# Attention with low parts and masks formed by adding transfers, and a reordered end, in a one-core encoder block

## The chip, the cores and the metric

The kernel runs on one core of a Trainium2 chip. The metric is the device time of one execution in microseconds; the time before is the median of three runs, and one further execution was profiled. The engines are named as in the profile: PE (TensorE) multiplies matrices, DVE (VectorE) and ACT (ScalarE) do elementwise work and can read PE's banks, POOL (GpSimd) does elementwise work on on-chip memory only and issues transfers, and SP issues transfers. All five run their own queue of instructions in a fixed order.

## The reference

One layer over 512 positions of width 1024, in float32. Cut to what matters here:

```python
h = rmsnorm(x, norm_mix_g);  z = h @ w_in           # u, v, q, k, v, f_logit, gates
a = gmlp_spatial_gating(z_u, z_v, ...)              # 8 groups
for i in range(4):                                  # query blocks of 128, 16 heads of 64
    s = q_i @ k[:hi].T * 64**-0.5 + cum_i[:, None] - cum[None, :hi]
    s = where(kpos <= qpos, s, -1e30)
    o_i = softmax(s) @ v[:hi]
x = x + (gate_a * (a @ w_branch_a) + gate_b * (o @ w_branch_b)) @ w_out
x = x + (gelu(conv(up)) * conv(up)) @ w_down        # gated MLP, causal depthwise conv
x = x + (p @ w_ple) * sigmoid(rmsnorm(x) @ w_ple_gate)
return rmsnorm(x, norm_final_g)
```

`cum` is the running sum of log sigmoid(f_logit + b_f) of each head.

## The kernel before

**Two parts for each operand.** PE multiplies in a reduced float32 (fp32r in the profile). Weights and activations are therefore split into a high part (`hi`, the value rounded by a copy on ACT) and a low part (`lo`, the value less its high part), and a product is three matmuls: lo x hi, hi x lo, hi x hi (`mm3`, L166 to L169, and `proj_T_steps`, L171 to L186). `load_w` (from L145) loads a weight piece of 128 x 1024 from HBM on SP's queue into a `raw` buffer, writes `hi` on ACT (L153), and forms `lo` in one of three ways: a subtraction on DVE (L159, the default), the same on POOL (`sub=G`), or `sub="dma"`: ACT writes minus `hi` into `lo` (L156), and a transfer that POOL issues adds `raw` to it (L157). There are three `raw` buffers and a ring of five `hi`/`lo` pairs. The up-projection uses the third way throughout.

**The order of the work.** PE's order is written out by hand in every stage: generators yield after each matmul, and `weave` mixes them. The other queues are filled by a scheduler that runs a model of the chip when the kernel is built; it takes an instruction when its inputs are there in the model, earlier ones first, and so can move one ahead of what stands in front of it in the program. Within `tc.manual_schedule(engines=...)` the engines named keep the order of the program.

**Attention.** Eight pairs of heads. In the pass for pair `pr`, PE interleaves three things: the transposes of that pair's probabilities and their product with v; the scores of pair `pr+1`; and, as filling, the projections of q and k for pair `pr+2` (two weight pieces) and those of one gate or, in the last pass, two (one weight piece each). For each head and query block, `softmax_head` lets PE form the scores in one of two `sc` banks, DVE adds the row of `cum` and takes the minimum (L849 for the diagonal block with the mask in `md`, L853 for the others with `cum`), and ACT takes the exponential (L856). DVE scales the four blocks of a head by the reciprocal sums (L863). `transpose_head` transposes them into one of three `pt` banks, from where ACT copies the high part `pth` (L380) and DVE forms the low part `ptl` (L381); the fourth transpose of a head needs the bank of the first. `cum_pair` loads the two rows of `cum` of a pair, spread over all 128 partitions, with one transfer on SP, and POOL adds the mask block (0 or 1e30) to a copy of all four key blocks, `md` (L831; one buffer for both heads). The low parts of the q and k weights of pairs 2 to 7 are formed on POOL, those of pairs 0 and 1, of the gates, and of the two first pieces of `w_branch_b` on DVE.

**The end.** The last stage multiplies by `w_ple_gate`, in two halves of the columns, four blocks of 128 rows each. `evac_gate` (L1313) follows each block: `add_ple` takes the sigmoid on ACT, multiplies and adds on DVE (L1297, L1298) and forms the sum of squares (L449 on ACT); POOL multiplies by the final gain (`times_g`, L1306). After the second half POOL adds the two sums (L1320), divides and adds epsilon (L1321) and finds the reciprocal root by three Newton steps (`rsqrt_of`, L397 to L403); ACT scales the low half of the row block (L1323), DVE the high half (L1324), and one transfer on SP stores it. The last row block's second half is cut into two of 256 columns; its root is taken on ACT with one Newton step on DVE (`rstd_of`, L386 to L390), its halves are scaled on ACT (L1360) and DVE (L1362) and stored from ACT's and SP's queues.

Of the kernel before, what the change touches and what calls it, by code (L numbers as in the profile page):

```python
# [15 lines left out]
P = 128  # L16
# [27 lines left out]
def hybrid_block(  # L44
# [338 lines left out]
    def rstd_of(ms, eps_scale):  # L383

        a, sd, y, t = tiny("ra"), tiny("rsd"), tiny("ry"), tiny("rt")
        A.activation(sd, ms, AF.Sqrt, scale=eps_scale, bias=epst)  # L386
# [3 lines left out]
        V.tensor_scalar(y, t, 1.5, y, ALU.add, ALU.mult)  # L390
        return y
# [262 lines left out]
    def gate_weights(n):  # L654
        return load_w(w_in_v[:, :, gate_col(n):gate_col(n) + P], 8, P)
# [13 lines left out]
    def qk_weights(pr):  # L669
        return [load_w(w_in_v[:, :, c0 + P * pr:c0 + P * pr + P], 8, P, sub=G if pr > 1 else V)  # L670
                for c0 in (2048, 3072)]
# [154 lines left out]
    def cum_pair(pr):  # L826
        cum = att.tile([P, 2, S], F32, tag="cum", name=uid("cum"), bufs=2)
        nc.sync.dma_start(cum, bass.AP(tensor=cum_d.tensor, offset=cum_d.offset + 2 * pr * S,
                                       ap=[[0, P], [S, 2], [1, S]]))
        md = att.tile([P, 2, S], F32, tag="md", name=uid("md"), bufs=1)  # L830
        G.tensor_tensor(md.rearrange("p a (n k) -> p (a n) k", k=P),  # L831
                        cum.rearrange("p a (n k) -> p (a n) k", k=P),
                        maskb[:, None, :].broadcast_to([P, 2 * NB, P]), ALU.add)
        return cum, md

    def softmax_head(qk, cm, a, probs):

        qs_, ks_, kh = qk
        cum, md = cm
        rs = tiny("rs", NB, bufs=4)  # L840
        for i in range(NB - 1, -1, -1):
            n = P * (i + 1)
            qs = slice(P * i, P * i + P)
            bk = bank("sc")
            T.matmul(bk[:, :n], qs_[:, a, qs], ks_[:, a, :n], start=True, stop=False)
            T.matmul(bk[:, :n], qs_[:, a, qs], kh[:, a, :n], start=False, stop=True)
            t = att.tile([P, n], F32, tag=f"t{i}", name=uid(f"t{i}"), bufs=T_BUFS)
            mn = tiny("mn", 2, bufs=8)
            V.tensor_tensor_reduce(t[:, n - P:], bk[:, n - P:n], md[:, a, n - P:n],  # L849
                                   1.0, 3e38, ALU.add, ALU.min, mn[:, 0:1])  # L850
            m = mn[:, 0:1]
            if i:
                V.tensor_tensor_reduce(t[:, :n - P], bk[:, :n - P], cum[:, a, :n - P],  # L853
                                       1.0, mn[:, 0:1], ALU.add, ALU.min, mn[:, 1:2])
# [40 lines left out]
    def gate_early(n):  # L895
        return gate_steps(n, "mm", lambda: att.tile([P, S], F32, tag="ot", name=uid("gt"), bufs=1))
# [391 lines left out]
    def add_ple(bk, rb, c, tag):  # L1288
# [13 lines left out]
        V.scalar_tensor_tensor(bk, xr, 1.0, xr, ALU.mult, ALU.mult, accum_out=ss)  # L1302
        return ss

    def times_g(eng, rb, c):
        eng.tensor_tensor(ple[:, rb, c], x1[:, rb, c], gfin[:, c], ALU.mult)  # L1306

# [5 lines left out]
    def evac_gate(bk, rb, ch):  # L1313
        if ch == 0:
            half[rb] = add_ple(bk, rb, lo_c, "s0")
            times_g(G, rb, lo_c)
            return
        ss = add_ple(bk, rb, hi_c, "s1")
        times_g(G, rb, hi_c)
        G.tensor_tensor(ss, ss, half[rb], ALU.add)  # L1320
        G.tensor_scalar(ss, ss, 1.0 / D, EPS, ALU.mult, ALU.add)  # L1321
        y = rsqrt_of(ss, eng=G)
        A.activation(ple[:, rb, lo_c], ple[:, rb, lo_c], AF.Copy, scale=y)  # L1323
        V.tensor_scalar(ple[:, rb, hi_c], ple[:, rb, hi_c], y, None, ALU.mult)  # L1324
        nc.sync.dma_start(out_rows(rb, slice(0, D)), ple[:, rb, :])

    with tc.manual_schedule(engines={mybir.EngineType.PE}):
# [15 lines left out]

        rb = NB - 1
        r = ds(rb * P, P)
        parts = []
        for c0 in (0, 256):
# [5 lines left out]
            parts.append(add_ple(bk, rb, c, f"s{2 + c0 // 256}"))  # L1353
            if c0 == 0:
                V.tensor_tensor(half[rb], half[rb], parts[0], ALU.add)
# [4 lines left out]
        A.activation(ple[:, rb, lo_c], ple[:, rb, lo_c], AF.Copy, scale=y)  # L1360
        nc.scalar.dma_start(out_rows(rb, lo_c), ple[:, rb, lo_c])
# [37 lines left out]
```

## Time and profile before

| | |
|---|---|
| Median of three runs | 946.94 us (946.75 to 947.03) |
| The profiled execution | 946.21 us |
| Its span, first to last instruction | 944.4 us |
| Mean granted TensorE clock | 0.996 |
| Busy: PE, DVE, ACT, POOL | 98%, 66%, 55%, 16% of the span |
| Chain that ended last: PE, DVE, ACT, POOL | 89%, 5%, 2%, 1% |

The profile was taken of one execution. A row of a timeline gives the start in us from the start of the span, the length in us, the engine, the line in the kernel, the operation, the tiles it writes and reads, its size, how many instructions were merged, and in brackets how long the engine stood idle before it and what ended that. PE's matmuls are pipelined and their ends are modelled, so rows of PE overlap. A row of the busy time by stretch gives the stretch, its length, and the busy time of each engine in it with the number of instructions. A row of a group gives the count, the busy time and the mean length in ns, then the idle time before and what ended it.

### The profile page before, as it was taken

What the parts mean: (1) busy time and instruction counts of PE and PEld (TensorE: products, weight loads), DVE (VectorE), ACT (ScalarE), POOL (GpSimd) and SP (SyncE); (2) the same over time, 40 slices, a digit from 0 to 9 for tenths busy, and PEclk for the clock granted to TensorE, in tenths of its full rate; (3) what the DMA queues carried; (4) which work ended last, traced back from release to release, by engine and by line L of the source; (5) the groups of instructions that cost most, each with busy time, mean ns of one, the idle gap of its engine ahead of it and who ended that gap; (6) DMA issues with size and microseconds to landing.
All of it is one profiled execution on the core that took longest, in us unless ns stands there. A gap on an engine that the chain in (4) does not pass through costs nothing.

```text
span 944.4 us, 11947 instructions
## 1 busy us (share of the span) xinstructions
PE 923.5 (98%) x4327; PEld 765.1 (81%) x4327; DVE 625.6 (66%) x1104; ACT 521.7 (55%) x846; POOL 155.3 (16%) x160
## 2 busy tenths in 40 slices
PE   7999999999999998999999999999999999999995
PEld 6878888888888887888888888888888888888785
DVE  6787899557777888424554647667666767554844
ACT  7654675466666666433524566555565645444533
POOL 4000001352222101000001511110111101103125
PEclk9999999999999999999999999999999999999998
DMA  9523273753333321199842497684957764973202
GB/s 343 161 89 114 76 195 107 238 157 96 97 99 98 109 96 62 55 312 370 268 155 68 149 239 169 163 206 100 222 141 166 199 156 103 233 229 112 68 1 89
DMA packets 106376, 144.30 MB, mean 153 GB/s; under 512 B 5957, under 2 KB 71677, under 8 KB 106317
## 3 DMA queue, kind: packets, MB, share of 16 engines
q1 hardware_dynamic: 97740, 113.62, 37.7%
q0 software_dynamic: 8432, 29.66, 14.7%
q8 instruction: 34, 0.56, 0.3%
q14 instruction: 26, 0.20, 0.1%
q10 hardware_dynamic: 144, 0.26, 0.1%
HBM read 107.84 MB, written 14.71 MB: 130 GB/s over the span
## 4 chain that ended last, share of the span: by engine, by line
PE 89%; DVE 5%; ACT 2%; POOL 1%; issue 1%; DMA 1%; SPq 0%; POOLq 0%; DVEq 0%
PE bank L181 17%; PE bank L185 17%; PE bank L183 17%; PE bank L1190 8%; PE bank L243 3%; PE bank L247 3%; PE bank L245 3%; PE bank L317 3%; PE bank L313 3%; PE bank L320 3%; PE bank L168 2%; PE bank L169 2%; PE bank L167 2%; PE bank L883 2%; PE bank L874 1%
## 5 line engine op out<-in xcount | busy, mean ns | idle before, releaser
L181 PE MATMUL bank<-slot,wlo 128*128 128x512 f32 (+1 forms) x688 | 273.2, 398 | 0.0
L183 PE MATMUL bank<-slot,whi 128*128 128x512 f32 (+1 forms) x688 | 267.2, 389 | 0.0
L185 PE MATMUL bank<-slot,whi 128*128 128x512 f32 (+1 forms) x688 | 266.9, 389 | 0.0
L185 PEld LDWEIGHTS bank<-slot,whi 128*128 128x128 f32 x688 | 129.2, 188 | 26.7
L153 ACT CAST whi<-raw 128x1024 fp32r<-128x1024 f32 x105 | 109.8, 1048 | 70.3 <-PE bank L185 23.4
L181 PEld LDWEIGHTS bank<-slot,wlo 128*128 128x128 f32 x688 | 129.5, 188 | 21.5
L183 PEld LDWEIGHTS bank<-slot,whi 128*128 128x128 f32 x688 | 129.7, 189 | 20.5 <-DVE slot L381 0.2
L159 DVE TENSOR_TENSOR wlo<-raw,whi 128x1024 fp32r<-128x1024 f32 x51 | 63.0, 1238 | 46.0 <-ACT whi L153 45.6
L159 POOL TENSOR_TENSOR wlo<-raw,whi 128x1024 fp32r<-128x1024 f32 x21 | 51.3, 2447 | 194.4 <-ACT whi L153 186.8
L157 POOL DMA_DIRECT2D wlo<-raw x33 | 28.7, 871 | 222.5 <-ACT wlo L156 124.0
L1190 PE MATMUL bank<-whi,slot 128*128 128x512 f32 x192 | 61.7, 389 | 0.0
L243 PE MATMUL bank<-whi,slot 128*128 128x512 f32 x136 | 53.6, 396 | 2.0 <-DVE slot L381 2.0
L247 PE MATMUL bank<-whi,slot 128*128 128x512 f32 x136 | 53.2, 391 | 0.0
L245 PE MATMUL bank<-wlo,slot 128*128 128x512 f32 x136 | 52.9, 390 | 0.0
L1106 DVE SCALAR_TENSOR_TENSOR ul<-bank,cvT,ul 128x511 f32<-128x511 f32 x22 | 16.5, 750 | 46.3 <-ACT ul L1105 46.3
L1190 PEld LDWEIGHTS bank<-whi,slot 128*128 128x128 f32 x192 | 36.1, 188 | 7.4
L856 ACT ACTIVATE t<-t,mn 128x512 f32<-128x512 f32 (+1 forms) x64 | 35.9, 562 | 10.3 <-DVE mn L853 7.5
L380 ACT CAST pth<-bank 128x512 fp32r<-128x512 f32 (+1 forms) x64 | 26.2, 428 | 24.8 <-PE bank L874 24.6
L265 DVE TENSOR_TENSOR wlo<-slot,whi 128x1024 fp32r<-128x1024 f32 x24 | 29.3, 1222 | 15.7 <-ACT whi L264 15.7
L169 PE MATMUL bank<-whi,slot 128*128 128x512 f32 (+1 forms) x104 | 38.8, 373 | 0.0
L168 PE MATMUL bank<-wlo,slot 128*128 128x512 f32 (+1 forms) x104 | 38.8, 373 | 0.0
L167 PE MATMUL bank<-whi,slot 128*128 128x512 f32 (+1 forms) x104 | 38.7, 374 | 0.0
(327 smaller groups left out, 1812.3 us busy)
## 6 DMA issues: line engine op xcount, KB each, us to landing
raw<-in_w_up_dram SPq DMA_DIRECT2D x44, 512.0 KB, 4.3
raw<-in_w_in_dram SPq DMA_DIRECT2D x36, 512.0 KB, 5.2
wlo<-raw POOLq DMA_DIRECT2D x33, 512.0 KB, 5.4
more<-in_w_in_dram SPq DMA_DIRECT2D x20, 512.0 KB, 8.3
slot<-in_w_down_dram SPq DMA_DIRECT2D x16, 512.0 KB, 3.5
cum<-cum_d SPq DMA_DIRECT2D x8, 512.0 KB, 4.1
raw<-in_w_branch_b_dram SPq DMA_DIRECT2D x8, 512.0 KB, 3.8
slot<-aT_d SPq DMA_DIRECT2D x4, 1024.0 KB, 11.2
```

The source lines that it names most:

```text
L153: A.copy(hi, raw)
L159: (sub or V).tensor_tensor(lo, raw, hi.bitcast(F32), ALU.subtract)
L167: T.matmul(out_ap, alo, bhi, start=start, stop=False)
L168: T.matmul(out_ap, ahi, blo, start=False, stop=False)
L169: T.matmul(out_ap, ahi, bhi, start=False, stop=stop)
L181: T.matmul(out_ap, wl, ah, start=(n == 0 and k == 0), stop=False)
L183: T.matmul(out_ap, wh, al, start=False, stop=False)
L185: T.matmul(out_ap, wh, ah, start=False, stop=end)
L243: T.matmul(bk, alo[:, k, r], wh, start=(k == 0), stop=False)
L245: T.matmul(bk, ahi[:, k, r], wl, start=False, stop=False)
L247: T.matmul(bk, ahi[:, k, r], wh, start=False, stop=(k == nk - 1))
L1190: T.matmul(bk, l, m, start=(fresh and k == 0 and n == 0), stop=(k == 1 and n == 2), skip_group_check=not fresh)
```

## The change

In attention, the low parts of the q and k weights of pairs 2 to 7, of the gates from number 6 on, and of the first two pieces of `w_branch_b` are formed by the third way of `load_w` (ACT and an adding transfer). The masked rows `md` are loaded like `cum`, one head at a time, and the mask block is added to them by a transfer that POOL issues; `cum` shrinks to the 384 columns that are read; both have three buffers of one head each. None of POOL's additions and subtractions is left in that stage.

At the end, epsilon and the division by 1024 move into the first half's work (the scale of ACT's square, the factor on DVE, one addition on POOL), so that POOL's L1321 goes. The scaling and the store of the third row block are taken out of `evac_gate` and put behind those of the last row block; both its halves are scaled on ACT and its store goes out on ACT's queue. The last row block's halves are both scaled on DVE, high half first, and stored on SP's queue; its product with the gain comes after its scale; its root takes the last partial sum and the rest as two operands, so that one addition goes. ACT and DVE keep the order of the program there.

```diff
@@ rstd_of
-        a, sd, y, t = tiny("ra"), tiny("rsd"), tiny("ry"), tiny("rt")
-        A.activation(sd, ms, AF.Sqrt, scale=eps_scale, bias=epst)
+        a = tiny("ra")
         V.tensor_scalar(a, ms, -0.5 * eps_scale, -0.5 * EPS, ALU.mult, ALU.add)
+        return newton(a, ms, eps_scale, epst)
+
+    def newton(a, ms, scale, bias):
+        sd, y, t = tiny("rsd"), tiny("ry"), tiny("rt")
+        A.activation(sd, ms, AF.Sqrt, scale=scale, bias=bias)
         V.reciprocal(y, sd)
@@ qk_weights
-        return [load_w(..., 8, P, sub=G if pr > 1 else V)
+        return [load_w(..., 8, P, "dma" if pr > 1 else None)
@@ cum_pair
-        cum = att.tile([P, 2, S], F32, tag="cum", name=uid("cum"), bufs=2)
-        nc.sync.dma_start(cum, bass.AP(tensor=cum_d.tensor, offset=cum_d.offset + 2 * pr * S,
-                                       ap=[[0, P], [S, 2], [1, S]]))
-        md = att.tile([P, 2, S], F32, tag="md", name=uid("md"), bufs=1)
-        G.tensor_tensor(md.rearrange("p a (n k) -> p (a n) k", k=P),
-                        cum.rearrange("p a (n k) -> p (a n) k", k=P),
-                        maskb[:, None, :].broadcast_to([P, 2 * NB, P]), ALU.add)
-        return cum, md
+        res = []
+        for h in (2 * pr, 2 * pr + 1):
+            cum = att.tile([P, S - P], F32, tag="cum", name=uid("cum"), bufs=3)
+            md = att.tile([P, S], F32, tag="md", name=uid("md"), bufs=3)
+            for t, n in ((md, S), (cum, S - P)):
+                nc.sync.dma_start(t, bass.AP(tensor=cum_d.tensor, offset=cum_d.offset + h * S,
+                                             ap=[[0, P], [1, n]]))
+            G.dma_start(md.rearrange("p (n k) -> p n k", k=P),
+                        maskb[:, None, :].broadcast_to([P, NB, P]), accum_op=ALU.add)
+            res.append((cum, md))
+        return res
@@ gate_early
+        w = gate_weights(n, "dma" if n >= GATES[0] else None)
@@ preload_merge
-        w_merge.append(gate_weights(N_GATES - 1))
-        w_merge.append(pieces_T(w_b_v, 0))
+        w_merge.append(gate_weights(N_GATES - 1, "dma"))
+        w_merge.append(pieces_T(w_b_v, 0, "dma"))
@@ add_ple
+        ss = tiny(f"s{c.start // 256}", bufs=4)
         if n == 512:
-            return square_sum(bk, xr, tag)
-        ss = tiny(tag, bufs=4)
-        V.scalar_tensor_tensor(bk, xr, 1.0, xr, ALU.mult, ALU.mult, accum_out=ss)
+            A.activation(bk, xr, AF.Square, scale=D ** -0.5, accum_out=ss)
+        else:
+            V.scalar_tensor_tensor(bk, xr, 1.0 / D, xr, ALU.mult, ALU.mult, accum_out=ss)
         return ss
@@ evac_gate
-            half[rb] = add_ple(bk, rb, lo_c, "s0")
+            half[rb] = add_ple(bk, rb, lo_c)
+            G.tensor_scalar(half[rb], half[rb], EPS, None, ALU.add)
             times_g(G, rb, lo_c)
             return
-        ss = add_ple(bk, rb, hi_c, "s1")
+        ss = add_ple(bk, rb, hi_c)
+        G.tensor_tensor(ss, ss, half[rb], ALU.add)
+        y = rsqrt_of(ss, eng=G)
         times_g(G, rb, hi_c)
-        G.tensor_tensor(ss, ss, half[rb], ALU.add)
-        G.tensor_scalar(ss, ss, 1.0 / D, EPS, ALU.mult, ALU.add)
-        y = rsqrt_of(ss, eng=G)
-        A.activation(ple[:, rb, lo_c], ple[:, rb, lo_c], AF.Copy, scale=y)
-        V.tensor_scalar(ple[:, rb, hi_c], ple[:, rb, hi_c], y, None, ALU.mult)
-        nc.sync.dma_start(out_rows(rb, slice(0, D)), ple[:, rb, :])
+
+        def close(engs=(A, V), queue=nc.sync):
+            for c, eng in zip((lo_c, hi_c), engs):
+                times_y(rb, c, y, eng)
+            queue.dma_start(out_rows(rb, slice(0, D)), ple[:, rb, :])
+        rest[rb] = close
+        if rb < NB - 2:
+            close()
@@ the last row block, now under manual_schedule(engines={ET.PE, ET.Activation, ET.DVE})
-        V.tensor_tensor(half[rb], half[rb], parts[1], ALU.add)
-        y = rstd_of(half[rb], 1.0 / D)
+        a = tiny("ra")
+        V.tensor_scalar(a, part, half[rb], -0.5, ALU.add, ALU.mult)
+        y = newton(a, part, 1.0, half[rb])
         times_g(V, rb, c)
-        A.activation(ple[:, rb, lo_c], ple[:, rb, lo_c], AF.Copy, scale=y)
-        nc.scalar.dma_start(out_rows(rb, lo_c), ple[:, rb, lo_c])
-        V.tensor_scalar(ple[:, rb, hi_c], ple[:, rb, hi_c], y, None, ALU.mult)
+        times_y(rb, hi_c, y, V)
         nc.sync.dma_start(out_rows(rb, hi_c), ple[:, rb, hi_c])
+        times_y(rb, lo_c, y, V)
+        nc.sync.dma_start(out_rows(rb, lo_c), ple[:, rb, lo_c])
+        rest[rb - 1]((A, A), nc.scalar)
```

`times_y` scales one half of a row block by the block's scale, on ACT or on DVE.

More of the change, by code (lines that the diff above doesn't have):

```diff
@@ L652, in gate_col, with gate_weights @@
         return (6160 if n < NK else 5136) + P * (n % NK)
-    def gate_weights(n):
-        return load_w(w_in_v[:, :, gate_col(n):gate_col(n) + P], 8, P)
+    def gate_weights(n, sub=None):
+        return load_w(w_in_v[:, :, gate_col(n):gate_col(n) + P], 8, P, sub)
     def gate_tile():
@@ L669, in qk_weights @@
     def qk_weights(pr):
[L670 removed]
+        return [load_w(w_in_v[:, :, c0 + P * pr:c0 + P * pr + P], 8, P, "dma" if pr > 1 else None)
                 for c0 in (2048, 3072)]
@@ L895, in gate_early @@
     def gate_early(n):
-        return gate_steps(n, "mm", lambda: att.tile([P, S], F32, tag="ot", name=uid("gt"), bufs=1))
+        w = gate_weights(n, "dma" if n >= GATES[0] else None)
+        yield from gate_steps(n, "mm", lambda: att.tile([P, S], F32, tag="ot", name=uid("gt"), bufs=1), w)
     qk = [[] for _ in range(NPAIR)]
@@ L1306, in times_g, with times_y @@
         eng.tensor_tensor(ple[:, rb, c], x1[:, rb, c], gfin[:, c], ALU.mult)
+    def times_y(rb, c, y, eng):
+        if eng is A:
+            A.activation(ple[:, rb, c], ple[:, rb, c], AF.Copy, scale=y)
+        else:
+            V.tensor_scalar(ple[:, rb, c], ple[:, rb, c], y, None, ALU.mult)
     def out_rows(rb, c):
@@ L1342, in hybrid_block @@
         steps(pg, 72)
+    with tc.manual_schedule(engines={ET.PE, ET.Activation, ET.DVE}):
         rb = NB - 1
         r = ds(rb * P, P)
-        parts = []
         for c0 in (0, 256):
```

12 lines of the change are left out of this document (6 added, 6 removed).

## The prediction

> **What bounds the kernel now.** I read the page first, then the busy time by stretch, then who TensorE (PE) waits for, then the instructions around each of its stops, and last the end of the run.
>
> ```profile
> PE 923.5 (98%) x4327; PEld 765.1 (81%) x4327; DVE 625.6 (66%) x1104; ACT 521.7 (55%) x846; POOL 155.3 (16%) x160
> ```
>
> PE is busy for 923.5 of the span of 944.4 us, and the change takes no work from it. Only its 20.9 us of idle time can be won, and only the part that lies in the stages that the change touches. By stretch (length, then busy time of PE, weight load, DVE, ACT and POOL; clock; DMA share and rate):
>
> ```profile
> 205.00:220.00 15.00, 14.34 (x73) 11.71 (x72) 12.18 (x34) 9.95 (x23) 7.21 (x3) 1.00 0.49 141
> 220.00:350.00 130.00, 130.00 (x676) 108.77 (x675) 101.58 (x291) 86.10 (x193) 31.38 (x13) 1.00 0.33 96
> 350.00:378.00 28.00, 25.09 (x136) 20.26 (x135) 23.59 (x74) 18.82 (x48) 2.76 (x3) 1.00 0.22 70
> 925.00:944.40 19.40, 9.18 (x64) 8.39 (x62) 9.38 (x27) 7.04 (x14) 9.47 (x20) 0.79 0.28 109
> ```
>
> Attention runs from about 197 to 380. In its long middle PE has no idle time, although DVE is at 78% and ACT at 66%. PE is idle 0.66 us as attention gets going, 2.91 us in its last pairs, and 10.2 us at the end of the run. What PE waits for in attention (total, times, longest), and the rows at the stops:
>
> ```profile
> PE bank L874 <- DVE ptl L381: 3.2, 3, 1.7
> ```
> ```profile
> 216.66 0.33 PE L874 MATMUL bank<-ident,t 128*128 128x128 f32 x1 [0.66 <-DVE ptl L381]
> ...
> 358.21 0.39 PE L846 MATMUL bank<-kz,st 128*128 128x512 f32 x1
> 358.44 0.39 PE L181 MATMUL bank<-slot,wlo 128*128 128x512 f32 x1
> 360.55 0.33 PE L874 MATMUL bank<-ident,t 128*128 128x128 f32 x1 [1.72 <-DVE ptl L381]
> ...
> 376.01 0.33 PE L874 MATMUL bank<-ident,t 128*128 128x128 f32 x1 [0.87 <-DVE ptl L381]
> ```
>
> All three are the fourth transpose of a head, which needs the bank of the first back: ACT has to copy it (pth) and DVE to form its low part (ptl). Matmuls start 0.23 us apart (358.21, 358.44) but are drawn 0.39 long, so a stop is 0.16 us longer than its idle time: 0.82, 1.88 and 1.03 us. The remaining 0.3 us of idle time in 350 to 378 are two short stops near 367 and 369.
>
> **Why DVE is late there.**
>
> ```profile
> 211.31 4.70 DVE L863 TENSOR_SCALAR t<-t,ri 128x512 f32<-128x512 f32 x4
> ...
> 354.96 2.83 DVE L863 TENSOR_SCALAR t<-t,ri 128x512 f32<-128x512 f32 x4
> 357.83 0.69 DVE L892 TENSOR_TENSOR slot<-bank,ot 64x512 f32<-64x512 f32 x1
> 358.55 1.22 DVE L159 TENSOR_TENSOR wlo<-raw,whi 128x1024 fp32r<-128x1024 f32 x1
> 359.81 0.69 DVE L381 TENSOR_TENSOR ptl<-bank,pth 128x512 fp32r<-128x512 f32 x1
> ...
> 364.85 1.27 DVE L863 TENSOR_SCALAR t<-t,ri 128x512 f32<-128x512 f32 x4
> ```
> ```profile
> 210.40 2.40 POOL L831 TENSOR_TENSOR md<-cum,maskb 128x1024 f32<-128x1024 f32 x1 [0.86 <-PE bank L846]
> 213.51 2.42 POOL L159 TENSOR_TENSOR wlo<-raw,whi 128x1024 fp32r<-128x1024 f32 x1 [0.71 <-ACT whi L153]
> ...
> 354.32 2.40 POOL L831 TENSOR_TENSOR md<-cum,maskb 128x1024 f32<-128x1024 f32 x1 [21.64 <-DVE mn L849]
> ```
>
> The four scalings of a head (L863) take 1.27 us together at 364.85, 4.70 at 211.31 and 2.83 at 354.96. In the slow cases POOL is adding the mask or subtracting a low part, and the scaling that meets it stands until POOL has finished. So at 211 the loss is 3.43 us, at 355 it is 1.56 us, and there one more weight's low part (1.22 us) stands ahead of the ptl that PE needs.
>
> **The change in attention.** What goes, and what an adding transfer costs where the up-projection already uses it:
>
> ```profile
> L159 DVE TENSOR_TENSOR wlo<-raw,whi x12: 1222/1225/1228, 201.4 to 374.0; 128x1024 fp32r<-128x1024 f32 x12
> ```
> ```profile
> L159 POOL TENSOR_TENSOR wlo<-raw,whi 128x1024 fp32r<-128x1024 f32 x12 | 29.0, 2417 | 71.9 <-ACT whi L153 64.4 <-DVE st L822 7.5
> L831 POOL TENSOR_TENSOR md<-cum,maskb 128x1024 f32<-128x1024 f32 x8 | 19.2, 2400 | 48.6 <-issue 24.5 <-DVE mn L849 21.6 <-DMA cum<-cum_d 1.6
> ```
> ```profile
> L156 ACT ACTIVATE wlo<-whi x33: 1040/1060/1064, 537.5 to 831.6; 128x1024 fp32r<-128x1024 f32 x33
> ```
> ```profile
> L157 POOL DMA_DIRECT2D wlo<-raw x33: 860/869/915, 539.1 to 833.0; - x33
> DMA to landing us min/median/max: 4.6/5.3/8.8
> ```
>
> POOL loses all 48.2 us of arithmetic (29.0 + 19.2). DVE loses about a dozen low parts (9 gates, the last gate, two pieces of w_b): 12 x 1.225 = 14.7 us. ACT gains a negated copy for each of 24 weights: 24 x 1.06 = 25.4 us. POOL gains 24 issues of 0.87 us and 16 for the masks.
>
> At 216 DVE goes from the scalings (211.31 + 4.70) straight to the ptl that PE waits for; 3.43 us earlier, and the stop of 0.82 us is gone. At 358 DVE is 1.56 + 1.22 = 2.78 us earlier, more than 1.88, but now ACT decides:
>
> ```profile
> 357.45 0.57 ACT L380 CAST pth<-bank 128x512 fp32r<-128x512 f32 x1
> ```
>
> pth ends at 358.02, ptl takes 0.69, so the bank is free at about 358.8, and PE wants it at 358.67: nearly nothing is left. If one negated copy slips in front of pth, 1.06 us stay. I take 1.5 of 1.88. At 376 the last L159 on DVE (it starts at 374.0) goes, 1.23 against a stop of 1.03; with the same doubt about ACT I take 0.8. Of the two short stops I take 0.2, since pair 6 without a projection beside it leaves DVE nearly as long as PE. Together 0.82 + 1.5 + 0.8 + 0.2 = **3.3 us** (bounds: 0.8 if ACT takes over everywhere but at 216, 4.4 if all five go).
>
> Costed at nothing in the middle: ACT. In 130 us it goes from 86.1 by about 18 (17 copies) to some 104, 80%, which is where DVE stands today without stopping PE; and DVE gets slack in return. Also at nothing: the longer way of a low part. Two ACT passes, an issue and a landing are 2.1 + 5.3 = 7.4 us against 2.3, but the ring holds five weights and each feeds 24 matmuls of 0.23 us, 5.4 us of PE alone. If that cover were gone, a weight could be up to 5 us late. SP's three more loads a pair find the DMA engines at a share of 0.33.
>
> What can cost something is the very first mask, which now is a load and then an adding transfer:
>
> ```profile
> 197.29 0.29 DVE L849 CUSTOM_DVE_ANT_0 t<-bank,md 128x128 f32<-128x128 f32 x1 [0.93 <-POOL md L831]
> ```
> ```profile
> 197.45 0.33 PE L845 MATMUL bank<-st,st 128*128 128x384 f32 x1
> ...
> 199.63 0.28 PE L845 MATMUL bank<-st,st 128*128 128x256 f32 x1
> ```
>
> DVE waits 0.93 us for the mask already; PE does not stop, because its third score step, at 199.63 (the second is at 197.45), is the first that needs a bank back, one L849 and one L853 on DVE after the mask, about 1 us. The mask may thus be 1.4 us later than now, at 198.7. I know the adding transfer only with 512 KB and rows of 4 KB (4.6 to 8.8 us to land); here it is 256 KB in pieces of 512 bytes. POOL's addition of 2.40 us ended as DVE began, so the load had landed by 194.9; the half-size load should land a microsecond or two sooner, 193 to 194.8. With 4.6 the mask is there at 197.6 to 199.4, with 8.8 at 201.8 to 203.6: a stop of 0 to 0.7, or of 3 to 5. A gain is excluded, as PE doesn't stop there now. I take 0.4, by the lower row, since half the bytes move. For later heads three buffers give the mask over a head of lead (the scalings of two heads in turn are 9.9 us apart, 354.96 and 364.85). [...]
>
> **The change at the end.**
>
> ```profile
> 936.25 0.14 DVE L1302 DVE_READ_ACCUMULATOR bank<-slot 128x1 f32 x1
> 936.25 0.42 DVE L1306 TENSOR_TENSOR slot<-slot,slot 128x256 f32<-128x256 f32 x1
> 937.55 0.48 DVE L1324 TENSOR_SCALAR slot<-slot,qy 128x512 f32<-128x512 f32 x1 [0.89 <-POOL qy L403]
> ...
> 939.00 0.21 DVE L390 TENSOR_SCALAR ry<-rt,ry 128x1 f32<-128x1 f32 x1
> ```
> ```profile
> 937.55 0.72 ACT L1323 ACTIVATE slot<-slot,qy 128x512 f32<-128x512 f32 x1 [1.43 <-POOL qy L403]
> 938.18 0.28 ACT L386 ACTIVATE rsd<-s,epst 128x1 f32<-128x1 f32 x1
> 939.25 0.72 ACT L1360 ACTIVATE slot<-slot,ry 128x512 f32<-128x512 f32 x1 [0.79 <-DVE ry L390]
> 940.00 0.37 ACTq L1361 DMA_DIRECT2D out_dram<-slot  x1
> ```
> ```profile
> 933.22 0.42 POOL L1321 TENSOR_SCALAR s<-s 128x1 f32<-128x1 f32 x1
> ```
>
> The last square sum is there at 936.39, but both engines then stand before the third block's scale, which POOL has ready at 937.5, and the root starts only at 938.18. Now the root starts at about 936.4; root to finished scale took 939.21 - 938.18 = 1.03; then follow, on DVE in written order, the product with g (0.42) and two halves (0.48 each): the high half's store goes out near 938.3, the last one near 938.8, against 940.00. The third block's halves now run one after the other on ACT, 2 x 0.72 after 937.5 less the 0.4 that L1321 took out of POOL's chain: its store goes out at 938.5 to 939.0. So the last issue comes 1.0 to 1.4 us sooner. I take **1.2 us**, bounds 0.7 (the 512 KB store of block 2, now last, lands later than a 256 KB one) and 1.5.
>
> Sum: -3.3 + 0.4 - 1.2 = -4.1 us, a span of 940.3. The profiled execution took 946.21 with a span of 944.4; the median is 946.94, 0.7 above it. I take the difference off the median: **942.8**.
>
> **Rivals.** *ACT takes DVE's place* in the last pairs: negated copies stand before pth. For it: ACT is at 18.82 of 28 there and each copy is 1.06 us; against: ACT has 9 us free. Attention then gives 1.1, the whole 1.1 + 1.2 = 2.3: 944.6.
>
> *The issues stand in DVE's way as the additions did.* The rows show a scaling held by POOL's arithmetic, none beside an issue. At 0.87 an issue is shorter than the 1.56 and 3.43 lost, so the stops at 216 and 358 would still go; but 40 issues fall where only 20 operations did, and one on the scalings of each of the last two heads costs 2 x 0.87: -4.1 + 1.7, 944.5. [...]
>
> *The first mask is late* as by the 8.8 us row: a stop of about 3 us, once: 945.4.
>
> *Slower*: POOL issues in order, and a mask's add queued behind a weight's add waits until ACT has made both passes, which wait until PE has left a ring slot. DVE's first minimum of the head then waits, and PE stops at its third score step. It decides once the mask comes so late that the step after the next (2.2 us apart, 197.45 and 199.63) finds no bank; with 1.3 us beyond that in each of seven pairs it is 9.1 - 4.5 = +4.6, 951.5. Against it: three buffers let the add be issued a head ahead.
>
> **How the numbers follow.** Forecast 0.62, ACT 0.12, issues 0.09, late first mask 0.10, slower 0.07. The measurement tells 0.2%, 1.9 us, from no change, so faster means under 945.0. The forecast and about half of the two middle cases are faster: 0.73; the other half and the late mask lie within: 0.20; slower 0.07. The range runs from all stops gone and the best end (-4.4 - 1.5, 941.0) to the weak bounds of both parts with the mask's 0.4 on top (-0.8 - 0.7 + 0.4, 945.8), past the late mask.
>
> **What would show it.** No POOL arithmetic between 190 and 380; L863 at 1.3 us for every head; PE's wait for ptl in attention under 1 us; ACT near 80% in the middle and PE still without idle time; the first L849 waiting under 2 us; the last square root at 936.4 less the shift, and the last store 2.5 us behind it. I am wrong if PE waits for pth, md or wlo in attention, or if the third block's scale still ends last.

## The result and the profile after

| | before | after |
|---|---|---|
| Median, us | 946.85 (946.51 to 947.03, 4 runs) | 983.27 (981.58 to 983.73, 4 runs) |
| The profiled execution, its span | 946.21, 944.4 | 981.58, 979.8 |
| Mean granted TensorE clock | 0.996 | 0.981 |

The ratio of after to before is 1.0382, with a 95% interval of 1.0364 to 1.04: the change makes the kernel slower, by 36 us. In the changed kernel the lines from attention on have moved: the mask's adding transfer is L840, the loads of `cum` and `md` are L837, the minima L858 and L862, the scalings L872, the transposes L883, the copy of an attention output L900. The first part of the profile's page of after:

```profile
PE 934.0 (95%) x4327; PEld 772.8 (79%) x4327; DVE 600.5 (61%) x1091; ACT 544.2 (56%) x870; POOL 149.8 (15%) x181
```

PE is busy for 10.5 us longer with the same 4327 matmuls, and idle for 45.8 us instead of 20.9: 10.5 + 24.9 is the 35.4 us by which the span grew. DVE lost 25 us of work and ACT gained 22; neither is the bound.

What PE waits for in attention (total, times, longest), and the rows at one of the stops:

```profile
PE bank L883 <- DVE ptl L381: 26.5, 6, 10.7
PE bank L854 <- DVE mn L862: 2.8, 1, 2.8
```
```profile
285.74 0.47 PE L883 MATMUL bank<-ident,t 128*128 128x128 f32 x1 [4.52 <-DVE ptl L381]
...
288.36 0.63 PE L183 MATMUL bank<-slot,whi 128*128 128x512 f32 x1
288.79 0.63 PE L185 MATMUL bank<-slot,whi 128*128 128x512 f32 x1
...
290.58 0.40 PE L185 MATMUL bank<-slot,whi 128*128 128x512 f32 x1
290.81 0.28 PE L854 MATMUL bank<-st,st 128*128 128x256 f32 x1
```

The wait is the one of before, at the fourth transpose of a head, but 26.5 us in place of 3.2, and it now comes once in nearly every pass. For a while after the stop the matmuls start 0.43 us apart (288.36, 288.79), later 0.23 (290.58, 290.81), as in the rows of before (358.21, 358.44).

Taking the same matmul in both traces, one can say where after falls behind. It starts attention 0.6 us late and loses 3.0 at the first mask. The stop at 216 goes, which gives back 0.8. Then the stops come: 1.4 us at 257, and 4.7, 4.3, 2.4 and 4.0 at 285.7, 316.0, 344.6 and 374.0, and 10.6 at 403. The stops are 28.5 to 30.3 us apart up to 374, where the same transposes were 24.0 apart before (252.65, 276.60, 300.54). Of the 36.3 us that PE is behind at its end another 8.6 are time at the slower clock. The forecast gains are in it as well: 0.8 at 216, 1.7 where 360.55 was, 1.0 where 376.01 was, some 3.5 in all.

**Who stands behind the late ptl.** What ACT, the queue of SP and POOL wait for between 190 and 425:

```profile
ACT ot L900 <- DMA gate_d<-gt: 19.8, 5, 11.3
ACT whi L153 <- DMA raw<-in_w_in_dram: 18.5, 5, 5.0
```
```profile
SPq L150 <- DMA wlo<-raw: 171.0, 24, 13.6
```
```profile
POOL md L840 <- DMA md<-cum_d: 67.3, 8, 12.6
```

SP stands for 171 us, 24 times, because the next weight's load needs a `raw` buffer from which an adding transfer still has to read; POOL stands for 67 us because a mask's load has not landed. The two wait for each other. The queues of SP, POOL and ACT ahead of the stop at 285.74, in their own order:

```profile
273.39 0.38 SPq L150 DMA_DIRECT2D raw<-in_w_in_dram  x1
273.87 1.25 SPq L837 DMA_DIRECT2D cum<-cum_d  x1
275.22 0.42 SPq L837 DMA_DIRECT2D md<-cum_d  x1
276.38 0.38 SPq L150 DMA_DIRECT2D raw<-in_w_in_dram  x1
276.85 0.53 SPq L671 DMA_DIRECT2D gate_d<-gt  x1
289.51 0.38 SPq L150 DMA_DIRECT2D raw<-in_w_in_dram  x1
```
```profile
281.96 1.42 POOL L840 DMA_DIRECT2D md<-maskb  x1 [12.52 <-DMA md<-cum_d]
282.89 1.40 POOL L157 DMA_DIRECT2D wlo<-raw  x1
```
```profile
278.21 1.05 ACT L153 CAST whi<-raw 128x1024 fp32r<-128x1024 f32 x1 [4.40 <-DMA raw<-in_w_in_dram]
...
283.77 0.58 ACT L900 COPY ot<-bank 64x512 f32<-64x512 f32 x1 [1.92 <-DMA gate_d<-gt]
284.38 1.24 ACT L380 CAST pth<-bank 128x512 fp32r<-128x512 f32 x3
```

At 273.39 SP gets a `raw` buffer (an adding transfer landed at 273.34) and issues a weight's load; behind it stand the loads of `cum` and `md`. POOL has stood for 12.52 us for that mask and issues its add at 281.96; behind it, in POOL's order, stands a weight's add, although its weight landed at 264.14 and ACT was done with it at 267.56. That add lands at 289.49, and at 289.51 SP gets the next `raw` buffer. This is one **trip**: weight load, mask load behind it, mask add, weight add behind it, the next weight load. It took 16.1 us, the next one 13.4 (to 302.93), and there are two in a pass, one for each head's mask. So a pass takes 29.5 us, while PE needs 24.0. PE notices through ACT, which in the order of its queue waits for the weight (4.40 us) and then, to copy an attention output into the only `ot` buffer, for the landing of the gate's store that stands behind a waiting load (1.92); `pth` and `ptl` come behind that.

**The end.** The scaling of the third row block, which waits for POOL's root, and the last store of after:

```profile
974.07 1.33 ACT L1321 ACTIVATE slot<-slot,qy 128x512 f32<-128x512 f32 x2 [1.25 <-POOL qy L407]
975.43 0.37 ACTq L1344 DMA_DIRECT2D out_dram<-slot  x1
```

PE's last matmul ends at 970.50, against 934.18 before, so the last store is issued 4.93 us behind it instead of 5.82, and the run ends 9.3 us behind it instead of 10.2: 1.0 us won. How much of that the stores won is taken up with the end alone, below.

### The profile page after: what moved, and what is told of

Its sections match the earlier page's. It is cut to its first block, busy times and chain, and to the rows that moved or that the text cites. A ratio compares the mean times of both kernels' runs of the same rounds, so it can differ in the third digit from the quotient of the medians.

```text
span 979.8 us, 12091 instructions
## 1 busy us (share of the span) xinstructions
PE 934.0 (95%) x4327; PEld 772.8 (79%) x4327; DVE 600.5 (61%) x1091; ACT 544.2 (56%) x870; POOL 149.8 (15%) x181
## 4 chain that ended last, share of the span: by engine, by line
PE 81%; DMA 9%; DVE 4%; ACT 3%; issue 1%; SPq 0%; POOL 0%; POOLq 0%; DVEq 0%; ACTq 0%
PE bank L181 15%; PE bank L183 15%; PE bank L185 15%; PE bank L1200 8%; PE bank L247 3%; PE bank L243 3%; PE bank L245 3%; DMA raw<-in_w_in_dram 3%; PE bank L320 3%; PE bank L313 3%; PE bank L317 3%; PE bank L168 2%; PE bank L169 2%; PE bank L167 2%; DMA wlo<-raw 2%; DMA gate_d<-gt 2%
## 5 line engine op out<-in xcount | busy, mean ns | idle before, releaser
L185 PEld LDWEIGHTS bank<-slot,whi 128*128 128x128 f32 x688 | 130.5, 190 | 27.0
L183 PEld LDWEIGHTS bank<-slot,whi 128*128 128x128 f32 x688 | 131.1, 191 | 20.7 <-DVE slot L381 0.2
L157 POOL DMA_DIRECT2D wlo<-raw x57 | 57.5, 1107 | 253.9 <-ACT wlo L156 118.5
L159 DVE TENSOR_TENSOR wlo<-raw,whi 128x1024 fp32r<-128x1024 f32 x39 | 48.3, 1242 | 45.7 <-ACT whi L153 45.5
L156 ACT ACTIVATE wlo<-whi 128x1024 fp32r<-128x1024 f32 x57 | 60.2, 1059 | 1.0
L883 PE MATMUL bank<-ident,t 128*128 128x128 f32 x160 | 28.7, 277 | 26.5 <-DVE ptl L381 26.5
L883 PEld LDWEIGHTS bank<-ident,t 128*128 128x128 f32 x160 | 21.1, 141 | 35.8 <-DVE ptl L381 29.4
L840 POOL DMA_DIRECT2D md<-maskb x16 | 21.0, 1314 | 149.4 <-DMA md<-cum_d 67.3
L159 POOL TENSOR_TENSOR wlo<-raw,whi 128x1024 fp32r<-128x1024 f32 x9 | 22.3, 2489 | 124.8 <-ACT whi L153 124.8
L858 DVE CUSTOM_DVE_ANT_0 t<-bank,md 128x128 f32<-128x128 f32 x64 | 18.4, 288 | 33.7 <-PE bank L855 28.0
```

Of the source, the lines that this page charges most:

```text
L156: A.activation(lo, hi.bitcast(F32), AF.Copy, scale=-1.0)
L157: G.dma_start(lo, raw, accum_op=ALU.add)
L159: (sub or V).tensor_tensor(lo, raw, hi.bitcast(F32), ALU.subtract)
L183: T.matmul(out_ap, wh, al, start=False, stop=False)
L185: T.matmul(out_ap, wh, ah, start=False, stop=end)
L883: T.transpose(bk[:, P * (i - j):P * (i - j) + P], probs[i][:, P * j:P * j + P], ident)
```

## The experiments

Theory, before the first run: the loop just described, of three `raw` buffers and two queues. Rivals: the adding transfers are slow in themselves or crowd the DMA engines; the late first mask sets everything off; the store of the gate alone holds ACT. The scheduler filled the queues anew for each variant, so more than the lines shown can have moved; what each one waits for is read from its own trace.

**The end alone**: attention as before.

```diff
@@ qk_weights; gate_early, preload_merge, cum_pair and softmax_head likewise as in the kernel before
-        return [load_w(..., 8, P, "dma" if pr > 1 else None)
+        return [load_w(..., 8, P, sub=G if pr > 1 else V)
```

> The end of the change alone; attention as before. Prediction's term: 1.2 us faster (bounds 0.7 and 1.5), so about 945.7. From the two traces the way from PE's last matmul to the end of the span went from 10.25 to 9.28 us, so 1.0 us: 945.9. If the end had a hand in the 36 us, it would be slower than before.

It took 946.92 us (11 runs) against 946.86 (21 runs), ratio 1.0001 (0.9992 to 1.001): nothing.

```profile
938.61 0.49 POOL L407 TENSOR_SCALAR qy<-qt,qy 128x1 f32<-128x1 f32 x1
```
```profile
940.50 0.37 ACTq L1339 DMA_DIRECT2D out_dram<-slot  x1
```

PE ends at 935.58 here, so the last issue is 4.92 us behind it, as in after, and the stores have landed at 7.95. But POOL, whose last arithmetic ends at 939.10, has a closing drain, the longest of the three drains that each of these rows counts (min, median and max in ns, then the first and last start in us; for before, for this run, and for after):

```profile
L1394 POOLq DRAIN  x3: 40/93/6457, 937.2 to 944.2; - x3
```
```profile
L1413 POOLq DRAIN  x3: 40/93/6686, 938.5 to 945.7; - x3
```
```profile
L1418 POOLq DRAIN  x3: 40/93/4727, 973.5 to 979.5; - x3
```

Here it runs from 2.97 to 9.66 us behind PE's end, and the run ends with it; SP's last waits, for the stores, are over at 8.52. The profiled run of before ended in the same way: its drain ends at 9.47, SP's last waits at 8.76. In after the drain ends at 7.71 and the stores decide, with SP's waits over at 8.52. So of the 1.0 us won at the end of after the stores account for 0.2, and the shorter drain for 0.7. In these three rows the drain lasts 6.46, 6.69 and 4.73 us. What sets its length was not tried.

**The weights by adding transfers, the masks by POOL as before**, with the new end.

```diff
@@ cum_pair; softmax_head likewise as in the kernel before
-            G.dma_start(md.rearrange("p (n k) -> p n k", k=P),
-                        maskb[:, None, :].broadcast_to([P, NB, P]), accum_op=ALU.add)
+        G.tensor_tensor(md.rearrange("p a (n k) -> p (a n) k", k=P),
+                        cum.rearrange("p a (n k) -> p (a n) k", k=P),
+                        maskb[:, None, :].broadcast_to([P, 2 * NB, P]), ALU.add)
```

> The end, and the weights' low parts by adding transfers; the masks by POOL's addition as before. Theory loop (a raw buffer is free only when its add has landed; SP's queue then holds the mask loads behind the waiting weight load, and POOL's queue holds the weights' adds behind the mask's add, so each waits for the other): without mask transfers the circle is cut, a raw buffer is held about 5 + 2 + 1 + 5 = 13 us of the 24 us of a pass, no stop once a pass; 944 to 945.5. Rival adds (the weights' adds or ACT's negated copies are too slow by themselves): most of the 36 us are here, over 965.

944.49 us (944.0 to 945.29, 10 runs), ratio 0.9975 (0.9966 to 0.9984): faster than before. The stretches of attention, as in the prediction:

```profile
205.00:220.00 15.00, 15.00 (x76) 12.55 (x75) 10.96 (x38) 11.85 (x25) 4.21 (x4) 1.00 0.91 220
220.00:350.00 130.00, 130.00 (x675) 108.88 (x675) 90.10 (x285) 100.57 (x211) 26.32 (x21) 1.00 0.67 165
350.00:378.00 28.00, 26.38 (x144) 21.74 (x143) 19.58 (x68) 20.56 (x49) 5.41 (x6) 1.00 0.48 123
```

PE has no idle time up to 350, with ACT at 100.57 of 130, and 1.62 us between 350 and 378 instead of 2.91. Here also SP's load of a weight waits for an adding transfer (145.8 us in 24 waits), without harm: POOL holds one mask operation a pass, and it waits for a mask's load only once, 4.4 us for the first.

**The masks by adding transfers, the weights as before**, with the new end.

```diff
-        return [load_w(..., 8, P, "dma" if pr > 1 else None)
+        return [load_w(..., 8, P, sub=G if pr > 1 else V)
@@ gate_early, preload_merge
-        w = gate_weights(n, "dma" if n >= GATES[0] else None)
+        w = gate_weights(n)
```

> The end, and the masks by adding transfers; the weights' low parts on DVE and POOL as before. Theory loop: raw buffers come free with the subtraction, so no circle; only the late first mask stays (3.5 us in the trace of the change), and the stop at 216 goes in part: 946 to 950. Rival masks (adds of 512-byte pieces are too slow by themselves): a stop of 3 to 5 us in each of seven passes, over 970.

947.44 us in one run beside 946.86. PE is 4.0 us behind before at the first mask, 1.6 of it from ahead of attention, and 2.2 at its end; no stop once a pass. So the masks' adding transfers do no harm alone. The weights' did none in the run before this one, but there a pair's mask comes by one load; the run head by head, below, shows that this matters.

**The loads of `cum` and `md` from ACT's queue**, all else as in the change.

```diff
-                nc.sync.dma_start(t, bass.AP(tensor=cum_d.tensor, ...
+                nc.scalar.dma_start(t, bass.AP(tensor=cum_d.tensor, ...
```

> The whole change, but the loads of cum and md are issued from ACT's queue in place of SP's. Theory loop: the mask no longer waits behind a weight load, the circle is cut; the late first mask stays and ACT pays some 2 us of issues a pass; 946 to 952. Rivals adds, masks and a rival store (the gate's store waits on SP and holds the one buffer that ACT's copy needs, whatever the masks do): the transfers are the same, over 970.

951.59 us in one run. What PE waits for in attention:

```profile
PE bank L854 <- DVE mn L862: 3.8, 2, 3.6
PE bank L883 <- DVE ptl L381: 1.4, 1, 1.4
```

```profile
SPq L150 <- DMA wlo<-raw: 167.5, 24, 13.1
```

Same transfers, same bytes, same three `raw` buffers, and SP's weight loads still wait 167.5 us for adding transfers; only the mask loads no longer stand behind loads that wait. Of 26.5 us of PE's waiting for `ptl` 1.4 are left, and about 32 of the 36 us go. What stays is the first mask: a stop of 3.6 us and 6.8 us at half clock behind it.

**A fourth `raw` buffer**: every fourth weight lands in a buffer of attention's own pool (one mask buffer less, for the room).

```diff
+    state["more"], state["x"] = att, 1
-            md = att.tile([P, S], F32, tag="md", name=uid("md"), bufs=3)
+            md = att.tile([P, S], F32, tag="md", name=uid("md"), bufs=2)
```

> The whole change with a fourth landing buffer for weights in the attention stage (4 KB; to make room the mask tiles have two buffers instead of three). Theory, the loop: a weight's load waits on SyncE for the landing of the adding transfer three weights ahead, and that add waits on GpSimd behind mask adds that wait for loads standing behind that weight's load. With four buffers the load waits for the add of four weights ahead, that is of the pass before, 7 to 9 us sooner than now: the stops once a pass shrink from 4 to 11 us to 0 to 2 and the run falls from 981.6 to 948 to 960. Rival, the order on GpSimd's queue alone (the masks' adds late whatever the landing buffers do): 977 to 985, since nothing on that queue changes.

974.18 us in one run: a miss for the theory as it stood, and under the rival's 977 as well.

SP still stands 164.6 us for adding transfers (122.5 for the three buffers of before, 42.1 for the new one). The trace shows why: the scheduler lets SP run one weight further ahead, and the mask loads again stand just behind the weight load that waits. The trips from 272.74 to 286.89, 299.93 and 315.68 are 14.2, 13.0 and 15.8 us long, still two a pass. So a fourth `raw` buffer does not open the loop. What it is worth alone this run does not show, since a mask buffer was given up for it.

**The gate's store from ACT's queue.**

```diff
-        yield from gate_steps(n, "mm", lambda: att.tile(..., tag="ot", ...), w)
+        yield from gate_steps(n, "mm", lambda: att.tile(..., tag="ot", ...), w, nc.scalar)
```

> The whole change with one line different: the store of a finished gate tile in attention goes out from ScalarE's queue, right behind the copy that makes the tile, instead of SyncE's. Theory, the loop of landing buffers: the store is no longer behind loads that wait, so the single gate tile is free sooner, but the weights' loads and the mask loads still wait for each other; most of the 36 us stay: 962 to 980. Rival, the store holds it all (ScalarE waits for the store's landing before it copies the next attention output, and every transposed tile behind it is late): the stops go with the store, 945 to 957.

980.42 us in one run. `ot` waits for the store only 11.0 us instead of 19.8, yet PE's wait for `ptl` is 25.0 instead of 26.5, and ACT still waits 23.0 for weights. The store passes the lateness on; it doesn't make it.

**Masks by transfer with the mask loads on ACT's queue, the first pair's mask by POOL's arithmetic.**

```diff
-            G.dma_start(mdv, mb, accum_op=ALU.add)
+            if pr == 0:  G.tensor_tensor(mdv, mdv, mb, ALU.add)
+            else:        G.dma_start(mdv, mb, accum_op=ALU.add)
-                nc.sync.dma_start(t, bass.AP(tensor=cum_d.tensor, ...
+                (nc.scalar if pr else nc.sync).dma_start(t, bass.AP(tensor=cum_d.tensor, ...
```

> The whole change with the mask loads of the second pair and later issued from ScalarE's queue, and the mask of the first pair added by GpSimd's arithmetic in place of the adding transfer. Theory: the loop is cut as in the run with all mask loads on ScalarE's queue (951.6), and the first mask's stop there (3.9 us, with its slower clock 7 in all) goes too: 944 to 948, equal to or slightly above the version with weights by transfers and masks by arithmetic (944.49), since the masks by transfer take ScalarE's time for six issues a pass and earn nothing. Rival, the masks by arithmetic still cost the version above its last 2.6 us of stops: 941 to 943.5.

945.4 us (944.03 to 948.66, 10 runs), ratio 0.9987 (0.9977 to 0.9996): the change with loop and first stop removed is a little faster than before. Adding the masks by transfer earned nothing here over adding them on POOL, pair by pair (944.49).

**The first pair's mask by arithmetic, all loads on SP.**

```diff
-            G.dma_start(mdv, mb, accum_op=ALU.add)
+            if pr == 0:  G.tensor_tensor(mdv, mdv, mb, ALU.add)
+            else:        G.dma_start(mdv, mb, accum_op=ALU.add)
```

> The whole change with only the first pair's two masks added by GpSimd's arithmetic (plain load, then an addition in place of 128 rows by 512), all other masks and the weights by transfers, all loads on SyncE as in the change. Theory: the first stop of 2.8 us and the slower clock behind it go, 3 to 5 us, and the loop of the later passes stays: 975 to 980. Rival, the late first mask sets the whole sequence off (without it the queues never fall behind): 944 to 952.

980.18 us in one run: 3.1 below the median of after. The first stop is gone, PE's wait for `ptl` is 28.7 us. The late first mask does not set off the loop.

**A fourth mask buffer.**

```diff
-            md = att.tile([P, S], F32, tag="md", name=uid("md"), bufs=3)
+            md = att.tile([P, S], F32, tag="md", name=uid("md"), bufs=4)
```

> The whole change with a fourth mask tile, so that a mask is loaded and added one head further ahead. After the miss with the fourth landing buffer the theory is narrower: in a pass SyncE's queue holds weight load, mask load, and again weight load, mask load; GpSimd's queue holds mask add, weight add, mask add, weight adds. A trip (weight load, mask load behind it, mask add, weight add behind it, the next weight load waiting for that landing) takes some 13 to 15 us, and there are two trips a pass, 29 us against the 24 that PE needs. A further buffer of either kind shifts both queues alike and leaves two trips a pass: 976 to 985, no better than the change. Rival, the masks are merely too late by some us: a head (12 us) of lead ends all stops, 945 to 960.

966.35 us in one run, between what the two theories expected. The loop stays in kind: from 273.61 to 288.48 to 301.03 are trips of 14.9 and 12.5 us, 27.4 a pass, and PE waits 12.0 us for `ptl` in five stops of up to 3.5. But the lead is worth 17 us: each stop is shorter, the stop of 10.7 us in the last pairs does not come, and less time falls into the slow clock. "No better than the change" was wrong.

**Weights by transfers, masks by POOL's arithmetic, but head by head** (128 by 512, in place) instead of pair by pair.

```diff
-            G.dma_start(md.rearrange("p (n k) -> p n k", k=P), maskb[...], accum_op=ALU.add)
+            G.tensor_tensor(mdv, mdv, maskb[:, None, :].broadcast_to([P, NB, P]), ALU.add)
```

> The version with weights by transfers and masks by GpSimd's arithmetic (944.49), with the masks loaded and added head by head in place (128 by 512) instead of pair by pair out of place (128 by 1024), so that an adding transfer for a weight stands behind half as long an operation on GpSimd. Theory: of the 2.6 us of stops left there between 358 and 385 about half goes: 942.8 to 944.5. Rival, those stops come from ScalarE's and VectorE's own order and not from GpSimd's: 944 to 945, no difference.

959.29 us (958.18 to 963.21, 5 runs), ratio 1.0141 (1.0123 to 1.016), 14.8 us slower than the version pair by pair: both expectations missed, and the loop stands without any adding transfer for a mask.

```profile
287.10 0.38 SPq L150 DMA_DIRECT2D raw<-in_w_in_dram  x1
287.58 1.71 SPq L837 DMA_DIRECT2D cum<-cum_d  x1
289.39 0.65 SPq L837 DMA_DIRECT2D md<-cum_d  x1
...
301.24 0.38 SPq L150 DMA_DIRECT2D raw<-in_w_in_dram  x1
```
```profile
295.38 1.29 POOL L841 TENSOR_TENSOR md<-md,maskb 128x512 f32<-128x512 f32 x1 [11.16 <-DMA md<-cum_d]
296.63 0.96 POOL L157 DMA_DIRECT2D wlo<-raw  x1
```

The columns are those of the timeline. POOL waits 11.16 us for the mask's load, adds it in 1.29, and the weight's add behind it lands at 301.23; at 301.24 SP goes on. Two trips a pass, 26 us. More differs from the version pair by pair than the size of the add: SP has four loads of `cum` and `md` a pair here instead of one of `cum`.

**One mask load and one adding transfer for both heads of a pair**, all else as in the change.

```diff
-        for h in (2 * pr, 2 * pr + 1):  md = att.tile([P, S], ..., bufs=3);  G.dma_start(md..., accum_op=ALU.add)
+        md = att.tile([P, 2, S], F32, tag="md", name=uid("md"), bufs=2)
+        G.dma_start(md.rearrange("p a (n k) -> p (a n) k", k=P),
+                    maskb[:, None, :].broadcast_to([P, 2 * NB, P]), accum_op=ALU.add)
```

> The whole change with one mask load and one adding transfer for both heads of a pair (128 by 1024, two buffers), nothing else moved. Theory of the two queues: that leaves one trip a pass instead of two; with some 5 us for the mask load, 3 for the issue of the longer mask add and 9 for the weight's add to land the trip is about 17 us, under the 24 that PE needs, and the stops once a pass go: 947 to 958, what is left being the first pair's mask (3 to 7 us with its slower clock; its longer add may make it somewhat later than in the change). Rival, it is the time of the transfers as such, or their number of bytes on the engines: those are the same, so 970 to 985.

953.84 us in one run. What PE waits for in attention:

```profile
PE bank L854 <- DVE mn L862: 5.4, 2, 5.2
PE bank L883 <- DVE ptl L381: 3.2, 2, 1.8
```

The same bytes for the masks, and as many adding transfers for weights: halving the number of trips ends the stops once a pass (26.5 to 3.2 us). Nearly all that is left is the first mask, 5.4 us late at PE and another 2.2 at half clock, as its add now covers both heads.

So the cause is shown. The stops once a pass go when one link of the loop is taken out (the masks' loads from SP's queue, or the weights' adds), or when a pair's mask comes by one load and one add, by a transfer or on POOL. They stay when POOL itself adds the masks head by head, so the masks' adding transfers are not a link of their own; they stay, smaller, with one buffer more, and they stay with the store or the first mask put elsewhere.

## Why the prediction was wrong

**The step that failed** is "Also at nothing: the longer way of a low part." It compared 7.4 us with 2.3 and named as cover that "the ring holds five weights". The ring holds `hi` and `lo`. What the adding transfer keeps is the `raw` buffer, of which there are three, and which the subtraction of before gave back 1.2 or 2.4 us after it began. The trip traced above shows a weight that landed at 264.14, whose add was issued at 282.89 and landed at 289.49: 25.4 us of a buffer, of which 15.3, from the end of ACT's passes at 267.56, were POOL's order. "If that cover were gone, a weight could be up to 5 us late" put a bound on one weight; a loop that takes 29.5 us where PE takes 24.0 loses that in every pass. The landings themselves were less far off (in attention, 190 to 425: KB each, median us to landing):

```profile
wlo<-raw POOLq DMA_DIRECT2D x24, 512.0 KB, 7.0
md<-maskb POOLq DMA_DIRECT2D x16, 256.0 KB, 4.3
```

**SP's queue.** "SP's three more loads a pair find the DMA engines at a share of 0.33" answered with bandwidth a question of order. The loads had to be moved past on SP's queue as well, and the masks' loads stand there behind a load that waits.

**The slower rival** had the right engine and the wrong order: a mask's add behind a weight's add. It is the weight's add behind the mask's that closes the loop. Its price, 1.3 us in each of seven pairs, was far too small, and PE stopped at the transposes, not at the third score step. "Against it: three buffers let the add be issued a head ahead" was false comfort: a fourth buffer still took 966.35.

**The first mask**: 0.4 forecast, 3.0 measured. The add landed 8.4 us after its issue, at the 8.8 us of the row that was set aside, and DVE waited 5.14 us for it:

```profile
193.50 1.32 POOL L840 DMA_DIRECT2D md<-maskb  x1 [2.10 <-DMA md<-cum_d]
```
```profile
202.07 0.29 DVE L858 CUSTOM_DVE_ANT_0 t<-bank,md 128x128 f32<-128x128 f32 x1 [5.14 <-DMA md<-maskb]
```

Halving the bytes gave the lower price only where the DMA engines were less busy. The DMA share, last but one in this row, was 1.15 while this mask's add was on its way, and 0.81 for the one issued at 281.96:

```profile
193.50:201.94 8.44, 6.87 (x31) 5.41 (x29) 1.38 (x2) 5.47 (x7) 3.91 (x4) 1.00 1.15 227
```

The first five masks, all at a share of 1.15 or more, took 5.7 to 8.4 us to land; the other eleven, at 0.87 or less, took 4.2 to 4.4.

**The gains of attention, 3.3 us, were right**, stop by stop: 0.8 of 0.82, 1.7 where 1.5 was taken, 1.0 where 0.8 was taken. They are there under the losses, and in the version with weights alone attention wins 1.9. ACT did not become the bound; in the stretch with the stops it is busy for 117.34 of 185 us:

```profile
220.00:405.00 185.00, 158.52 (x778) 131.03 (x777) 99.65 (x339) 117.34 (x248) 33.20 (x31) 0.92 0.82 169
```

**The rival of the issues.** The four scalings of a head take 1.27 or 1.28 us in 13 of 16 heads, and 1.43, 1.63 and 1.63 in the others:

```profile
282.09 1.63 DVE L872 TENSOR_SCALAR t<-t,ri 128x512 f32<-128x512 f32 x4
...
341.93 1.27 DVE L872 TENSOR_SCALAR t<-t,ri 128x512 f32<-128x512 f32 x4
```
```profile
340.43 1.29 POOL L840 DMA_DIRECT2D md<-maskb  x1 [12.63 <-DMA md<-cum_d]
341.18 1.64 POOL L157 DMA_DIRECT2D wlo<-raw  x1
```

The one at 282.09 lies beside a mask's issue (281.96 to 283.38) and takes 0.36 longer, and the two other long ones lie beside a mask's issue too; the one at 341.93 lies beside a weight's issue and takes none. These rows show a loss of 0.36 us at most.

**The end** was wrong as well, and its size came out near by luck: 1.2 forecast, 1.0 in the changed kernel. The prediction took the issue of the last store for the end of the run. That issue came 0.9 us sooner (4.93 against 5.82 us behind PE), but it is now that of the larger store, the third block's (512 KB, 3.0 us from issue to landing), and SP's last waits end only 0.2 sooner. In the trace of before POOL's closing drain, for which the prediction has no term, ended the run 0.7 us behind those waits (9.47 against 8.76); in after the drain is shorter, and that is most of the 1.0. Alone the new end was worth 0.0, since there the drain ends 1.1 us behind SP's last waits (9.66 against 8.52).

## What to carry to other kernels

Here an adding transfer kept the `raw` buffer that it reads until it landed (at 289.49; the next load was issued at 289.51). So count the buffers at the source as well as at the destination, and then write down the queues in their own order: the weight load that waited for that buffer held the loads of `cum` and `md` behind it on SP's queue to 289.98 and 290.62. Where two queues wait for each other, price the whole trip and compare it with the time of a pass; a further mask buffer only made the stops shorter here (966.35 us), while one trip fewer (953.84), or the masks' loads on another queue (951.59), ended those that come once a pass. Of this change the part to keep is the weights' low parts by adding transfers with the masks left on POOL, pair by pair: 944.49 us.

## What the hardware showed unexpectedly

**A stop of PE costs more than its length.** The clock has two values here, by stretch (length, busy times, then the clock):

```profile
276.50:283.30 6.80, 4.72 (x26) 3.55 (x24) 2.08 (x5) 3.59 (x7) 1.34 (x2) 1.00 0.87 230
283.30:290.10 6.80, 4.36 (x12) 3.59 (x13) 4.93 (x16) 6.06 (x12) 0.99 (x2) 0.50 0.77 117
290.10:296.90 6.80, 6.80 (x39) 5.80 (x38) 3.80 (x13) 4.39 (x11) 1.04 (x2) 1.00 0.49 145
```

Every stretch at half clock in attention is 3.41 us long or two or three times that: five of them in after, 30.7 us together, 8.6 us lost. A stop of 2.81 us at the first mask of after brought none, one of 2.55 at the same place, with the store moved, brought 3.41 us of half clock, and so did the one of 2.20 that ends at 344.56 in after. The two stops at the first mask differ in where they lie. In after the edges of the half-clock stretches of attention lie on one grid of 3.41 us. The stop of 2.81 us falls into two steps of that grid, 1.03 us into the one from 197.99 and 1.78 into the next; with the store moved, 2.45 of the 2.55 us lie in the 3.40 us from 200.0, which half clock followed (0.50 from 203.4 to 206.8). In after, from 20 to 925 us, five steps at full clock had 1.96 us or more without a matmul (those from 279.91, 310.63, 341.35, 372.07 and 392.55, with 2.10, 2.17, 2.20, 1.96 and 3.37), and half clock followed each; the next longest, from 368.65 with 1.79 us, was followed by full clock. In the trace of before the clock stayed full from 20 to 925 us; PE stands idle there for 1.72 us at the longest.

**Adding transfers of the same size landed anywhere from 4.2 to 8.4 us after their issue** (the 16 masks of after, 256 KB each). A weight's issue on POOL that follows a mask's closely is drawn 1.45 us long there in place of 0.86, but its row begins before the other's ends: the one drawn from 201.37 to 202.82 ends only 0.91 us behind the mask's, drawn from 200.62 to 201.91.
